# Modulation vectors from transposed weights: row sums on VectorE in place of sums over partitions on TensorE

## The chip, the cores and the metric

The kernel runs on one NeuronCore of a Trainium2 chip (the 1 core that the program uses). The metric is the time of one execution on the device in microseconds. TensorE (PE in the rows) multiplies matrices; its weight loads (PEld) overlap its matmuls. VectorE (DVE) and ScalarE (ACT) work elementwise, GpSimd (POOL) does small work beside them, and SyncE (SP) issues nearly all transfers, in the order of its queue.

## What is computed

A diffusion backbone of two layers over 1024 latent tokens and 256 context tokens of width 1024, all in float32. Each layer has a mixer (attention and spatial gating side by side) and a SwiGLU FFN. What matters here is the modulation: from a condition `c` for the latent tokens and `c_ctx` for the context tokens each layer computes six vectors of 1024, which scale, shift and gate the two sub-layers.

```python
silu_c, silu_cc = silu(c), silu(c_ctx)
for l in range(2):
    m_x = (silu_c  @ w_mod[l] + b_mod[l]).reshape(6, 1024)   # w_mod[l]: 1024 x 6144
    m_c = (silu_cc @ w_mod[l] + b_mod[l]).reshape(6, 1024)
    hx = rms_norm(x, g_pre_mix[l]) * (1 + m_x[1]) + m_x[0]   # scale 1, shift 0
    hc = rms_norm(xc, g_pre_mix[l]) * (1 + m_c[1]) + m_c[0]
    x  = x + m_x[2] * rms_norm(mixer(hx, hc), g_post_mix[l]) # gate 2
    x  = x + m_x[5] * rms_norm(ffn(rms_norm(x, g_pre_ffn[l]) * (1 + m_x[4]) + m_x[3]), g_post_ffn[l])
```

The context stream goes the same way with `m_c`; it is not needed behind the mixer's keys and values in the second layer.

## The kernel before

Activations stand transposed, features on the partitions, as eight blocks (`KT`) of 128x128 for a tile of 128 tokens. Float32 products are made of three matmuls of rounded high and low parts: `rnd` (line 118) rounds a part on ScalarE, `sub_lo` (line 121) and `split_w` (line 377) take the remainder on VectorE. A page (`PG`, 35 of them) is 4 KB of every partition; `BK` are the eight banks of PSUM. A tile's name in the rows ends in `_p` for a page, `_b` for a buffer of four pages and `_k` for a bank.

The vectors for scale and shift must end as columns, in `fm[:, l, v, ...]`: feature on the partition, one column per block, with `v` 0 for latent and 1 for context. The gates must end as rows in device memory, from where they are later spread over all partitions (`load_g`).

The weights `w_mod` lie with the input feature on the partition. `mods_first` (line 169) makes shift and scale of the first layer's mixer before anything else can start: the scale's eight blocks, and one of the shift's, go through TensorE with the two conditions as a two-column stationary operand (two rows in the bank, tile `m_k`); the other seven blocks of the shift are multiplied and added up by VectorE in two accumulators (`macc`, 128 partial sums per feature), and four matmuls with `one_v` sum these over the partitions. Four matmuls of one row put the bias in. The rows are then copied to `mrow`, transposed (`mt_k`) and put into `fm`.

All other vectors are made beside the main work by `mods_steps` (line 224), one job per vector, for one condition or both. A job takes a step when the main loops call `fill`: one weight block of 512 KB is loaded and multiplied by VectorE with a scalar per partition and added to the accumulator (line 235). At the end TensorE sums over the partitions, in tile `mg_k`: for a gate two matmuls of 512 columns with a column of ones as stationary operand, for scale and shift eight matmuls that load the accumulator's 128x128 blocks as weights and multiply them with the column of ones. Float32 matmuls take two passes each. The products' scheduling priority is put back (`late=150`), so that they run where VectorE has room. Jobs of both conditions are the gates and the first mixer vectors of each layer; in the first product of an FFN (`ffn_in`) the jobs have a ring of four pages to themselves (`rings["j"]`, line 1200).

At the start, `norm_early` normalises the two context tiles and transposes them; `norm_late` applies scale and shift (`hte` to `hTc`, high and low). `load_z` brings the first projection's weights (`wraw` to `winh`, `winl`), whose matmuls are `pz_k`. The latent tiles follow in four pairs: `norm_x` (`xs`), eight transposes a tile (`hT_k`), scale and shift (`ht`, line 342), high and low part (`hTl`). In the order of each engine's queue a scheduler decides, by dependencies, priorities and its own costs.

Of the kernel before, what the change touches and what calls it, by code (L numbers as in the profile page):

```python
# [10 lines left out]
F32 = mybir.dt.float32  # L11
F32R = mybir.dt.float32r
I32 = mybir.dt.int32
AF = mybir.ActivationFunctionType
# [18 lines left out]
NDVE = 7  # L33
# [62 lines left out]
def trunk(ctx: ExitStack, tc, x, xctx, w_mod, b_mod, vecs, gqk, gsg, g_post, w_z, w_in, w_sT, w_out,  # L96
# [14 lines left out]
    def mm(o, lhsT, rhs, start, stop):  # L111
        nc.tensor.matmul(o, lhsT, rhs, start=start, stop=stop)  # L112

    def act(o, i, f, **kw):
        A.activation(out=o, in_=i, func=f, **kw)  # L115
# [18 lines left out]
    one_v = cst.tile([P, 2, 2], F32, name="one_v")  # L134
    nc.gpsimd.memset(one_v, 0.0)
    for v in range(2):
        nc.gpsimd.memset(one_v[:, v, v:v + 1], 1.0)
    one2 = cst.tile([1, 2], F32, name="one2")
    nc.gpsimd.memset(one2, 1.0)
# [4 lines left out]
    dma(out=vrow.t[:64, :], in_=vecs)  # L144
    bk = BK.get([512], F32, "vt")
# [4 lines left out]
    act(cT.rearrange("p a b -> p (a b)"), vec[:, 48:64], AF.Silu)  # L150

# [10 lines left out]
    def put_scale(l, v, ffn, src):  # L162
        V.scalar_tensor_tensor(out=fm[:, l, v, 2 * ffn, :], in0=src, scalar=1.0, in1=gpre(l, ffn),
                               op0=ALU.add, op1=ALU.mult)

    def put_shift(l, v, ffn, src):
        V.tensor_copy(out=fm[:, l, v, 2 * ffn + 1, :], in_=src)

    def mods_first():

        parts = (1, 0)
        bks = [[BK.get([512], F32, "m0") for _ in range(2)] for _ in parts]
        row = PG.get([1024], F32, "mrow")
        nc.gpsimd.memset(row.t[:34, :], 0.0)
        for n, p in enumerate(parts):
            b = PG.get([1024], F32, "brow")
            dma(out=b.t[:1, :], in_=b_mod[0, p * D:(p + 1) * D].partition_broadcast(1))
            for h in range(2):
                mm(bks[n][h].t[:2, :], one2, b.t[:1, h * 512:(h + 1) * 512], True, False)
            b.free()  # L180
        accs = [PG.get([1024], F32, "macc") for _ in range(2)]
        for kt in range(KT):
            if kt == NDVE:
                for v in range(2):
                    for h in range(2):
                        mm(bks[1][h].t[:2, :], one_v[:, v, :], accs[v].t[:, h * 512:(h + 1) * 512], False, False)
                    accs[v].free()
            for n, p in enumerate(parts):
                w = PG.get([1024], F32, "wm")
                dma(out=w.t, in_=w_mod[0, kt * P:(kt + 1) * P, p * D:(p + 1) * D])  # L190
                if p == 0 and kt < NDVE:
                    for v in range(2):
                        if kt == 0:
                            V.tensor_scalar(out=accs[v].t, in0=w.t, scalar1=cT[:, v, 0:1], scalar2=None, op0=ALU.mult)
                            continue
                        V.scalar_tensor_tensor(out=accs[v].t, in0=w.t, scalar=cT[:, v, kt:kt + 1], in1=accs[v].t,
                                               op0=ALU.mult, op1=ALU.add)
                else:
                    for h in range(2):
                        mm(bks[n][h].t[:2, :], cT[:, :, kt], w.t[:, h * 512:(h + 1) * 512], False, kt == KT - 1)  # L200
                w.free()
        yield
        with tc.high_priority():
            for n in range(2):
                for h in range(2):
                    o, i = row.t[32 * n:32 * n + 2, h * 512:(h + 1) * 512], bks[n][h].t[:2, :]
                    if h:
                        V.tensor_copy(out=o, in_=i)
                    else:
                        act(o, i, AF.Copy)  # L210
                    bks[n][h].free()
        bt = BK.get([KT, 34], F32, "mt")
        for k in range(KT):
            nc.tensor.transpose(bt.t[:, k, :], row.t[:34, k * P:(k + 1) * P], idn[:34, :34])
        row.free()
        for v in range(2):
            put_scale(0, v, 0, bt.t[:, :, v])
            put_shift(0, v, 0, bt.t[:, :, 32 + v])
        bt.free()
        yield  # L220
# [3 lines left out]
    def mods_steps(l, part, vs, late=150):  # L224
        accs = {}
# [4 lines left out]
        for kt in range(KT):  # L230
            w = jring[0].get([1024], F32, "wm")
            dma(out=w.t, in_=w_mod[l, kt * P:(kt + 1) * P, part * D:(part + 1) * D])
            with tc.high_priority(offset=-late):
                for v in vs:
                    V.scalar_tensor_tensor(out=accs[v].t, in0=w.t, scalar=cT[:, v, kt:kt + 1], in1=accs[v].t,  # L235
                                           op0=ALU.mult, op1=ALU.add)
            w.free()
            yield
        for _ in range(3):
            yield  # L240
        for v in vs:
            if part in (2, 5):
                g = jring[0].get([1024], F32, "gp")
                dma(out=g.t[0:1, :], in_=g_post[l, part // 5, :].partition_broadcast(1))
                for h in range(2):
                    bk = BK.get([512], F32, "mg")
                    mm(bk.t[0:1, :], ones[:, 0:1], accs[v].t[:, h * 512:(h + 1) * 512], True, True)
                    V.scalar_tensor_tensor(out=g.t[0:1, h * 512:(h + 1) * 512], in0=bk.t[0:1, :], scalar=32.0,
                                           in1=g.t[0:1, h * 512:(h + 1) * 512], op0=ALU.mult, op1=ALU.mult)
                    bk.free()  # L250
                d = dr.tile([1, D], F32, name=f"grow{l}{part}{v}")
                dma(out=d, in_=g.t[0:1, :])
                grow[l, part, v] = d
                g.free()
            else:
                bk = BK.get([512], F32, "mg")
# [3 lines left out]
                bk.free()  # L260
            accs[v].free()
        yield
# [39 lines left out]
    def norm_early(xt):  # L302

        xs = norm_x(xt)
# [146 lines left out]
    def gmlp_ln(vp, c0, sgrow, res):  # L451
# [3 lines left out]
        for c in range(2):  # L455
            st = sm.tile([P, 2, 6], F32, name="bnst", tag="bnst")
# [59 lines left out]
    def layer(l):  # L516
# [7 lines left out]
        if not last:  # L524
            hT.make_c()
            early = []
            for i in range(NC):
                xt = load_x(xc_d[i])
                early.append(norm_early(xt.t))
                xt.free()  # L530
            first = mods_first()
            next(first)
            wu += load_z(l, 0, (0, 1))
            next(first)
# [1102 lines left out]
def _layout(inputs):  # L1637
# [12 lines left out]
    w_in = w_in[:, :, 1024:].reshape(DEPTH, KT, P, NPIECE, PC).transpose(0, 3, 2, 1, 4)  # L1650
    w_fi = a["w_ffn_in"].reshape(DEPTH, KT, P, 2, NJ // 2, 2, P).transpose(0, 4, 3, 2, 5, 1, 6)
# [4 lines left out]
        "x": a["x"][0], "xctx": a["ctx"][0], "w_mod": a["w_mod"], "b_mod": a["b_mod"], "vecs": vecs, "gqk": gqk,  # L1656
        "gsg": np.stack([a["g_sg"], a["b_sg"]], 1), "g_post": np.stack([a["g_post_mix"], a["g_post_ffn"]], 1),
# [21 lines left out]
```

## Time and profile before

| what | us |
|---|---|
| median of 3 runs | 2685.35 |
| lowest and highest of them | 2679.77, 2685.67 |
| profiled execution, its own time | 2682.48 |
| its span | 2680.7 |
| TensorE busy (share of the span) | 2631.3 (98%) |
| weight loads of TensorE | 2163.6 (81%) |
| VectorE busy | 2044.2 (76%) |
| ScalarE busy | 1300.0 (48%) |
| GpSimd busy | 642.1 (24%) |

The profile is of one execution. Its span leaves out 1.8 us of its own time. The shares are means over stretches that differ: the start up to about 61 us waits for weights; the mixer, the FFN's first product (from about 680 to 1150 us in the first layer, from 2048 to 2458 in the second) and the FFN's second product follow one another. A matmul's row shows its latency; how many go through is seen from the distance of their starts. Where times are read from a stretch, they are times from the span's start.

### The profile page before, as it was taken

The numbers are of one execution on the slowest core, as the hardware profiler recorded it, in microseconds if no ns is written. First come the engines' busy times: TensorE is split into PE (matmuls) and PEld (weight loads), VectorE is DVE, ScalarE is ACT, GpSimd is POOL, SyncE is SP. The second block draws the span as 40 slices with busy tenths as digits, with TensorE's granted clock in tenths as the row PEclk, the third lists the DMA queues.
The fourth block names the chain that finished last, engine by engine and source line by source line (L and its number), as shares of the span: only waits on it lengthen the run. The fifth ranks groups of instructions, "written<-read, shape, count | busy, mean of one in ns | idle before, by whom it ended". The sixth has DMA issues, their size and how long they took to land. (4 is left out here: it accounts for less than half of the span.)

```text
span 2680.7 us, 35573 instructions
## 1 busy us (share of the span) xinstructions
PE 2631.3 (98%) x13125; PEld 2163.6 (81%) x13125; DVE 2044.2 (76%) x2886; ACT 1300.0 (48%) x2269; POOL 642.1 (24%) x637
## 2 busy tenths in 40 slices
PE   7999999999999999999999999999998999999998
PEld 4789777788888788888899889777787888888886
DVE  7775788857888887677898777888758766667776
ACT  5323788844332323543566323788745333334433
POOL 1112000002233333275010113000014223231746
PEclk9999999999999999999999999999999999999999
DMA  7430001233533333787576631001231422216984
GB/s 291 126 120 33 3 15 28 60 121 115 176 142 141 132 126 134 221 187 201 189 240 210 235 112 64 5 9 48 84 134 79 140 88 95 91 69 207 201 207 173
DMA packets 126458, 338.44 MB, mean 126 GB/s; under 512 B 24302, under 2 KB 25134, under 8 KB 121164
## 3 DMA queue, kind: packets, MB, share of 16 engines
q1 hardware_dynamic: 113612, 313.09, 34.1%
q0 software_dynamic: 12672, 23.07, 5.2%
q8 instruction: 103, 1.69, 0.3%
q14 instruction: 71, 0.58, 0.1%
HBM read 290.32 MB, written 45.71 MB: 125 GB/s over the span
## 5 line engine op out<-in xcount | busy, mean ns | idle before, releaser
L112 PE MATMUL fi_k<-blk_p,fw_p 128*128 128x512 f32 x2640 | 609.3, 390 | 0.7 <-ACT blk_p L118 0.7
L112 PEld LDWEIGHTS fi_k<-blk_p,fw_p 128*128 128x128 f32 x2640 | 496.6, 188 | 106.4 <-issue 1.7
L112 PE MATMUL fo_k<-fs_p,fs_p 128*128 128x512 f32 x1848 | 420.1, 389 | 0.2 <-DVE fs_p L121 0.2
L112 PEld LDWEIGHTS fo_k<-fs_p,fs_p 128*128 128x128 f32 x1848 | 346.6, 188 | 72.5 <-DVE fs_p L121 0.6
L118 ACT ACTIVATE fw_p<-fir_b 128x512 fp32r<-128x512 f32 x200 | 126.0, 631 | 318.4 <-PE fi_k L112 302.3
L112 PE MATMUL pv_k<-sp_b,vt_p 128*128 128x512 f32 (+3 forms) x1008 | 277.4, 392 | 2.8 <-DVE sp_b L121 2.0
L112 PE MATMUL fi_k<-blk_b,fw_p 128*128 128x512 f32 x1056 | 249.1, 392 | 1.1 <-DVE y_p L997 1.1
L121 DVE TENSOR_TENSOR fs_p<-fo_p,fs_p 128x512 fp32r<-128x512 f32 x212 | 191.5, 960 | 60.3 <-ACT fs_p L118 59.6
L112 PEld LDWEIGHTS fi_k<-blk_b,fw_p 128*128 128x128 f32 x1056 | 199.4, 189 | 43.0 <-DVE y_p L997 1.5
L287 POOL TENSOR_SCALAR rs<-ss 128x1 f32<-128x1 f32 x74 | 25.2, 340 | 870.1 <-DVE ss L993 594.4
L121 DVE TENSOR_TENSOR sp_b<-pt_p,sp_b 128x1024 fp32r<-128x1024 f32 (+1 forms) x168 | 200.4, 1196 | 23.1 <-ACT sp_b L118 20.4
L112 PEld LDWEIGHTS pv_k<-sp_b,vt_p 128*128 128x128 f32 (+1 forms) x1008 | 161.7, 170 | 58.2 <-DVE sp_b L121 8.0
L739 DVE TENSOR_REDUCE mx<-ml_k 128x1 f32<-128x512 f32 x256 | 169.1, 685 | 37.3 <-PE ml_k L112 36.6
L118 ACT ACTIVATE fs_p<-fo_p 128x512 fp32r<-128x512 f32 x212 | 119.4, 621 | 144.8 <-POOL fo_p L1273 55.3
L115 ACT ACTIVATE pt_p<-st_k 128x512 f32<-128x512 f32 (+1 forms) x336 | 180.6, 592 | 12.6 <-PE st_k L112 11.4
L121 DVE TENSOR_TENSOR fw_p<-fir_b,fw_p 128x512 fp32r<-128x512 f32 x200 | 178.1, 891 | 10.8 <-ACT fw_p L118 8.6
L235 DVE SCALAR_TENSOR_TENSOR macc_p<-wm_p,cT,macc_p 128x1024 f32<-128x1024 f32 x128 | 171.5, 1358 | 18.5 <-DMA wm_p<-in_w_mod_dram 15.8
L118 ACT ACTIVATE sp_b<-pt_p 128x1024 fp32r<-128x1024 f32 (+1 forms) x168 | 175.9, 1048 | 1.4
L112 PE MATMUL pz_k<-winh_p,hTl_b 128*128 128x512 f32 x512 | 160.7, 391 | 1.8 <-ACT hTl_b L118 1.2
L1110 POOL TENSOR_TENSOR S_p<-fir_b 128x512 f32<-128x512 f32 x40 | 58.1, 1453 | 376.2 <-issue 323.1
L112 PE MATMUL fi_k<-h2c_p,fih_p 128*128 128x256 f32 x704 | 128.0, 284 | 0.0
L112 PEld LDWEIGHTS pz_k<-winh_p,hTl_b 128*128 128x128 f32 x512 | 96.0, 188 | 25.2 <-issue 1.7
(275 smaller groups left out, 5045.8 us busy)
## 6 DMA issues: line engine op xcount, KB each, us to landing
wm_p<-in_w_mod_dram SPq DMA_DIRECT2D x112, 512.0 KB
fir_b<-in_w_fi_dram SPq DMA_DIRECT2D x40, 1024.0 KB
fir_p<-in_w_fi_dram SPq DMA_DIRECT2D x52, 512.0 KB
hid<-hid_p SPq DMA_DIRECT2D x44, 512.0 KB
fo_p<-hid SPq DMA_DIRECT2D x76, 256.0 KB
fo_p<-in_w_fo_dram SPq DMA_DIRECT2D x76, 256.0 KB
fo_p<-in_w_fo_dram POOLq DMA_DIRECT2D x74, 256.0 KB, 6.6
fo_b<-hid SPq DMA_DIRECT2D x56, 256.0 KB
```

The source lines that it names most:

```text
L112: nc.tensor.matmul(o, lhsT, rhs, start=start, stop=stop)
L115: A.activation(out=o, in_=i, func=f, **kw)
L118: A.activation(out=o, in_=i, func=AF.Copy)
L121: V.tensor_tensor(out=o, in0=i, in1=hi.bitcast(F32), op=ALU.subtract)
L235: V.scalar_tensor_tensor(out=accs[v].t, in0=w.t, scalar=cT[:, v, kt:kt + 1], in1=accs[v].t, op0=ALU.mult, op1=ALU.add)
L287: nc.gpsimd.tensor_scalar(out=y, in0=src, scalar1=float(eps), scalar2=1.0, op0=ALU.add, op1=ALU.mult)
L739: V.tensor_reduce(out=mx[:, b, i:i + 1], in_=bk.t, axis=AX.X, op=ALU.max)
L1110: tt_(out=sp.t[:, 0], in0=a21, in1=a22, op=ALU.add)
```

## The change

The weights are laid out transposed by the host: in block `[l, part, k]` the partition is the output feature and the 1024 inputs lie along the row. A condition's silu is spread as a row over all partitions (`crow`). One VectorE operation multiplies a weight block with that row and writes the sum along the row as one column (`accum_out`), straight into `fm` or, for a gate, into the column tile `gcol`. Nothing is left to sum over the partitions.

- `mods_steps`: no accumulator, no memset on GpSimd, no matmuls with ones. The bias, and for a gate also the post-norm's weight, come as columns (`load_cols`, tile `bcol`) and are added by one or two small VectorE operations. A gate's eight columns go through one transpose (128x8 to 8x128, `mg_k`) to become rows for device memory. Each job loads the silu row from device memory to all partitions, 512 KB per condition. With both conditions, the first product of a block goes to a page `prod` of its own and the second overwrites the weight block.
- `mods_first`: the scale's eight blocks stay on TensorE (`w_m1`, laid out as before). Of the shift, six blocks of outputs go to VectorE; two blocks of outputs (`NPE`, 256 columns) go to TensorE in eight matmuls (`w_m0`). The one-row matmuls and those with `one_v` are gone. The silu rows are loaded ahead of all else and passed to device memory for the jobs.
- The transposes of the context tiles, which stood among the two-row matmuls, now come after them (`tc.issue_after`): the first tile's, then those of `mrow`, then the second tile's.
- `bnst` has two buffers in place of four.

```diff
-NDVE = 7
+NPE = 2
@@ trunk
+    crow = [PG.get([1024], F32, "crow") for _ in range(2)]
+    for v in range(2):
+        dma(out=crow[v].t, in_=vecs[48 + 8 * v:56 + 8 * v, :].rearrange("a b -> (a b)").partition_broadcast(P))
...
+    cd = dr.tile([2, D], F32, name="crow")
+    for v in range(2):
+        act(crow[v].t, crow[v].t, AF.Silu)
@@ helpers
+    def load_cols(o, n=1):
+        b = sm.tile([P, 2, KT], F32, name="bcol", tag="bcol", bufs=2)
+        dma(out=b[:, :n], in_=cols[o:o + n].rearrange("n p k -> p n k"))
+        return b
...
+    def mods_block(ring, w, cr, res):
+        for n, c in enumerate(cr):
+            prod = w if n == len(cr) - 1 else ring.get([1024], F32, "prod")
+            V.scalar_tensor_tensor(out=prod.t, in0=w.t, scalar=1.0, in1=c.t, op0=ALU.mult, op1=ALU.mult, accum_out=res[n])
+            if prod is not w:
+                prod.free()
+        w.free()
@@ mods_first
...
+        for kt in range(KT):
+            w = PG.get([1024], F32, "wm")
+            dma(out=w.t, in_=w_m1[kt])
             for h in range(2):
+                mm(bks[h].t[:2, :], cT[:, :, kt], w.t[:, h * 512:(h + 1) * 512], kt == 0, kt == KT - 1)
+            w.free()
+            if kt < KT - NPE:
                 w = PG.get([1024], F32, "wm")
+                dma(out=w.t, in_=w_mod[0, 0, NPE + kt])
+                mods_block(PG, w, crow, [fm[:, 0, v, 1, NPE + kt:NPE + kt + 1] for v in range(2)])
+            elif kt < KT - NPE + 2:
+                o = 4 * (kt - KT + NPE)
+                w = PG.get([4, NPE * P], F32, "wm")
+                dma(out=w.t, in_=w_m0[:, o:o + 4])
+                for k in range(4):
+                    ins = mm(bs_.t[:2, :], cT[:, :, o + k], w.t[:, k], o + k == 0, o + k == KT - 1)
+                w.free()
+        for v in range(2):
+            dma(out=cd[v:v + 1, :], in_=crow[v].t[0:1, :])
+            crow[v].free()
+        yield ins
@@ mods_steps
         for v in vs:
-            accs[v] = jring[0].get([1024], F32, "macc")
-            nc.gpsimd.memset(accs[v].t, 0.0)
-            dma(out=accs[v].t[0:1, :], in_=b_mod[l, part * D:(part + 1) * D].partition_broadcast(1))
-        for kt in range(KT):
+            c = jring[0].get([1024], F32, "crow")
+            dma(out=c.t, in_=cd[v, :].partition_broadcast(P))
+            cr.append(c)
...
             w = jring[0].get([1024], F32, "wm")
-            dma(out=w.t, in_=w_mod[l, kt * P:(kt + 1) * P, part * D:(part + 1) * D])
+            dma(out=w.t, in_=w_mod[l, part, k])
             with tc.high_priority(offset=-late):
-                for v in vs:
-                    V.scalar_tensor_tensor(out=accs[v].t, in0=w.t, scalar=cT[:, v, kt:kt + 1], in1=accs[v].t,
-                                           op0=ALU.mult, op1=ALU.add)
-            w.free()
+                mods_block(jring[0], w, cr, [r[:, k:k + 1] for r in res])
...
             if part in (2, 5):
-                    mm(bk.t[0:1, :], ones[:, 0:1], accs[v].t[:, h * 512:(h + 1) * 512], True, True)
...
+                V.tensor_tensor(out=src, in0=src, in1=b[:, 0], op=ALU.add)
+                V.scalar_tensor_tensor(out=src, in0=src, scalar=32.0, in1=b[:, 1], op0=ALU.mult, op1=ALU.mult)
+                bk = BK.get([P], F32, "mg")
+                nc.tensor.transpose(bk.t[:KT, :], src, idn)
...
             else:
-                for k in range(KT):
-                    mm(bk.t[:, k:k + 1], accs[v].t[:, k * P:(k + 1) * P], ones[:, 0:1], True, True)
-                (put_shift if part in (0, 3) else put_scale)(l, v, part // 3, bk.t[:, :KT])
+                (put_shift if part in (0, 3) else put_scale)(l, v, part // 3, src, b[:, 0])
@@ layer
+            with tc.issue_after(ins.ins):
+                early = [norm_early(xcs[0])]
+                next(first)
+                early.append(norm_early(xcs[1]))
```

On VectorE in the first mixer, before the third pair of latent tiles (`ht_p_622`) gets its scale and shift, this stood before. `macc_p_528` and `macc_p_531` are the accumulators of the first gate; six more products of that gate stand ahead of the first pair.

```order
L235 SCALAR_TENSOR_TENSOR macc_p_528<-wm_p_546,cT,macc_p_528 128x1024
L235 SCALAR_TENSOR_TENSOR macc_p_531<-wm_p_546,cT,macc_p_531 128x1024
L235 SCALAR_TENSOR_TENSOR macc_p_528<-wm_p_664,cT,macc_p_528 128x1024
L235 SCALAR_TENSOR_TENSOR macc_p_531<-wm_p_664,cT,macc_p_531 128x1024
L235 SCALAR_TENSOR_TENSOR macc_p_528<-wm_p_668,cT,macc_p_528 128x1024
L299 TENSOR_SCALAR xs_p_684<-x_p_682,rs 128x1024
L299 TENSOR_SCALAR xs_p_693<-x_p_691,rs 128x1024
L235 SCALAR_TENSOR_TENSOR macc_p_528<-wm_p_672,cT,macc_p_528 128x1024
L235 SCALAR_TENSOR_TENSOR macc_p_531<-wm_p_668,cT,macc_p_531 128x1024
L235 SCALAR_TENSOR_TENSOR macc_p_528<-wm_p_676,cT,macc_p_528 128x1024
L235 SCALAR_TENSOR_TENSOR macc_p_531<-wm_p_672,cT,macc_p_531 128x1024
L235 SCALAR_TENSOR_TENSOR macc_p_531<-wm_p_676,cT,macc_p_531 128x1024
```

At the same place on VectorE stands now this; the third pair's first tile is `ht_p_628`, `crow_p_531` and `crow_p_533` are the silu rows of the two conditions, and two more products stand right ahead of this, two ahead of the first pair.

```order
L180 SCALAR_TENSOR_TENSOR prod_p_548,gcol<-wm_p_546,crow_p_531 128x1024
L180 SCALAR_TENSOR_TENSOR prod_p_553,gcol<-wm_p_551,crow_p_531 128x1024
L180 SCALAR_TENSOR_TENSOR wm_p_546,gcol<-wm_p_546,crow_p_533 128x1024
L180 SCALAR_TENSOR_TENSOR wm_p_551,gcol<-wm_p_551,crow_p_533 128x1024
L180 SCALAR_TENSOR_TENSOR prod_p_672,gcol<-wm_p_670,crow_p_531 128x1024
L180 SCALAR_TENSOR_TENSOR prod_p_677,gcol<-wm_p_675,crow_p_531 128x1024
L180 SCALAR_TENSOR_TENSOR wm_p_670,gcol<-wm_p_670,crow_p_533 128x1024
L180 SCALAR_TENSOR_TENSOR prod_p_682,gcol<-wm_p_680,crow_p_531 128x1024
L180 SCALAR_TENSOR_TENSOR wm_p_675,gcol<-wm_p_675,crow_p_533 128x1024
L312 TENSOR_SCALAR xs_p_694<-x_p_692,rs 128x1024
L180 SCALAR_TENSOR_TENSOR wm_p_680,gcol<-wm_p_680,crow_p_533 128x1024
L180 SCALAR_TENSOR_TENSOR prod_p_687,gcol<-wm_p_685,crow_p_531 128x1024
```

Ten of the sixteen products stood between the second pair and the third before; now it is thirteen, of which these are eleven.

On VectorE again, behind the third pair, before: the last operations of the fourth pair (`ht_p_775`) and the weight splits of the second projection.

```order
L121 TENSOR_TENSOR hTl_b_295<-ht_p_754,hTl_b_295 128x1024
L342 TENSOR_SCALAR ht_p_775<-hT_k_776,fm 128x128
L342 TENSOR_SCALAR ht_p_775<-hT_k_785,fm 128x128 x2
L248 SCALAR_TENSOR_TENSOR gp_p_796<-mg_k_798,gp_p_796 1x512
L377 TENSOR_TENSOR winl_p_888<-wraw_p_885,winh_p_887 128x1024
L121 TENSOR_TENSOR hTl_b_295<-ht_p_775,hTl_b_295 128x1024
L377 TENSOR_TENSOR winl_p_894<-wraw_p_891,winh_p_893 128x1024
L235 SCALAR_TENSOR_TENSOR macc_p_870<-wm_p_873,cT,macc_p_870 128x1024
```

Now, with `ht_p_785` as the fourth pair's last tile and `crow_p_878` as the silu row of the next job:

```order
L262 TENSOR_TENSOR gcol<-gcol,bcol 128x8
L389 TENSOR_TENSOR winl_p_895<-wraw_p_892,winh_p_894 128x1024
L263 SCALAR_TENSOR_TENSOR gcol<-gcol,bcol 128x8
L389 TENSOR_TENSOR winl_p_901<-wraw_p_898,winh_p_900 128x1024
L180 SCALAR_TENSOR_TENSOR wm_p_880,fm<-wm_p_880,crow_p_878 128x1024
L180 SCALAR_TENSOR_TENSOR wm_p_883,fm<-wm_p_883,crow_p_878 128x1024
L180 SCALAR_TENSOR_TENSOR wm_p_886,fm<-wm_p_886,crow_p_878 128x1024
L267 COPY gp_p_812<-mg_k_810 8x128
L354 TENSOR_SCALAR ht_p_785<-hT_k_795,fm 128x128 x2
L267 COPY gp_p_820<-mg_k_818 8x128
L180 SCALAR_TENSOR_TENSOR wm_p_889,fm<-wm_p_889,crow_p_878 128x1024
L121 TENSOR_TENSOR hTl_b_298<-ht_p_785,hTl_b_298 128x1024
```

Where one weight split stood ahead of the last tile's low part, two stand now, and four products of the next job.

## Rows read from the trace of the kernel before

**Rows 1.** The page, busy time of each engine (share of the span), xinstructions.

```profile
PE 2631.3 (98%) x13125; PEld 2163.6 (81%) x13125; DVE 2044.2 (76%) x2886; ACT 1300.0 (48%) x2269; POOL 642.1 (24%) x637
```

**Rows 2.** Busy time by stretch: PE, PEld, DVE, ACT, POOL; clock, DMA share, GB/s.

```profile
61.00:104.00 43.00, 42.42 (x191) 32.08 (x191) 39.84 (x55) 25.05 (x52) 5.81 (x9) 1.00 0.47 150
...
700.00:1060.00 360.00, 360.00 (x1615) 297.19 (x1614) 305.80 (x367) 108.55 (x180) 122.42 (x78) 0.99 0.40 141
1440.00:1700.00 260.00, 259.37 (x1711) 235.01 (x1710) 194.49 (x319) 101.46 (x184) 40.23 (x55) 1.00 0.39 131
2077.00:2141.00 64.00, 64.00 (x283) 52.67 (x283) 50.33 (x64) 21.74 (x37) 18.91 (x13) 1.00 0.38 132
```

**Rows 3.** The tile macc: xcount, duration ns min/median/max, first and last start.

```profile
L112 PEld LDWEIGHTS mg_k<-ones,macc_p x160: 186/192/338, 148.3 to 1642.8; 128*128 128x128 f32 x160
...
L235 DVE SCALAR_TENSOR_TENSOR macc_p<-wm_p,cT,macc_p x128: 1264/1279/2321, 49.3 to 2102.6; 128x1024 f32<-128x1024 f32 x128
...
L112 PE MATMUL mg_k<-macc_p,ones x24: 590/592/593, 87.0 to 2142.1; 128*1 128x512 f32 x24
L228 POOL MEMSET macc_p<- x16: 945/954/961, 32.1 to 2079.9; 128x1024 f32 x16
...
L196 DVE SCALAR_TENSOR_TENSOR macc_p<-wm_p,cT,macc_p x12: 1278/1282/1286, 13.1 to 27.1; 128x1024 f32<-128x1024 f32 x12
```

**Rows 4.** Timeline of PE around one scale group and one gate: start, us, operation.

```profile
147.59 0.62 PE L112 MATMUL pz_k<-winh_p,hTl_b 128*128 128x512 f32 x2
...
148.27 0.39 PE L112 MATMUL pz_k<-winh_p,hTl_b 128*128 128x512 f32 x1
148.50 1.84 PE L112 MATMUL mg_k<-ones,macc_p 128*128 128x1 f32 x16
150.20 0.49 PE L112 MATMUL pz_k<-winh_p,hTl_b 128*128 128x512 f32 x1
...
2140.84 1.88 PE L112 MATMUL mg_k<-macc_p,ones 128*1 128x512 f32 x4
2142.65 2.60 PE L112 MATMUL fi_k<-blk_p,fw_p 128*128 128x512 f32 x10
```

**Rows 5.** Timelines of DVE and PE, the latent tiles of the first mixer.

```profile
51.11 6.06 DVE L235 SCALAR_TENSOR_TENSOR macc_p<-wm_p,cT,macc_p 128x1024 f32<-128x1024 f32 x5
...
60.47 0.50 PE L112 MATMUL pz_k<-winh_p,hTl_b 128*128 128x512 f32 x1 [1.21 <-ACT hTl_b L118]
...
83.20 3.88 PE L335 MATMUL hT_k<-idr,xs_p 128*128 128x128 f32 x32
...
84.94 2.00 DVE L342 TENSOR_SCALAR ht_p<-hT_k,fm 128x128 f32<-128x128 f32 x6
...
95.02 1.20 DVE L377 TENSOR_TENSOR winl_p<-wraw_p,winh_p 128x1024 fp32r<-128x1024 f32 x1
```

**Rows 6.** Timeline of all engines, the start.

```profile
6.55 0.19 ACT L115 ACTIVATION_READ_ACCUMULATOR xs_p<-x_p 128x1 f32 x1
...
10.77 0.60 ACT L115 ACTIVATE hte_p<-hT_k 128x512 f32<-128x512 f32 x1
...
15.87 13.88 PE L112 MATMUL m_k<-wm_p,cT 128*2 128x512 f32 x28
...
29.68 1.06 ACT L118 ACTIVATE winh_p<-wraw_p 128x1024 fp32r<-128x1024 f32 x1 [15.77 <-DMA wraw_p<-in_w_z_dram]
...
33.02 3.60 PE L112 MATMUL m_k<-wm_p,cT 128*2 128x512 f32 x8
...
41.62 0.79 PE L112 MATMUL pz_k<-winh_p,hTc_p 128*128 128x512 f32 x1 [3.48 <-ACT hTc_p L118]
```

**Rows 7.** Busy time by stretch, columns as in rows 2, two pieces of the start.

```profile
16.00:18.00 2.00, 2.00 (x4) 0.34 (x3) 2.00 (x2) 0.00 (x0) 0.00 (x0) 0.64 1.03 418
18.00:20.00 2.00, 2.00 (x3) 0.26 (x2) 1.92 (x3) 0.00 (x0) 0.00 (x0) 0.51 1.02 406
```

**Rows 8.** Waits of the SP queue from 640 to 1150 us: total, times, longest.

```profile
SPq L232 <- DVE macc_p L235: 82.1, 29, 5.8
```

More of the change, by code (lines that the diff above doesn't have):

```diff
@@ L111, in mm @@
     def mm(o, lhsT, rhs, start, stop):
-        nc.tensor.matmul(o, lhsT, rhs, start=start, stop=stop)
+        return nc.tensor.matmul(o, lhsT, rhs, start=start, stop=stop)
     def act(o, i, f, **kw):
@@ L133, in trunk @@
     nc.gpsimd.memset(mhalf, -0.5)
[L134 to L139, printed above, removed]
     vec = cst.tile([P, 64], F32, name="vec")
@@ L169, in mods_first @@
     def mods_first():
-        parts = (1, 0)
-        bks = [[BK.get([512], F32, "m0") for _ in range(2)] for _ in parts]
+        bks = [BK.get([512], F32, "m0") for _ in range(2)]
+        bs_ = BK.get([NPE * P], F32, "m0")
         row = PG.get([1024], F32, "mrow")
         nc.gpsimd.memset(row.t[:34, :], 0.0)
-        for n, p in enumerate(parts):
-            b = PG.get([1024], F32, "brow")
-            dma(out=b.t[:1, :], in_=b_mod[0, p * D:(p + 1) * D].partition_broadcast(1))
+        b0 = load_cols(0, 2)
@@ L202, in mods_first @@
[L202 to L211, printed above, removed]
+                mm(bks[h].t[:2, :], cT[:, :, kt], w.t[:, h * 512:(h + 1) * 512], kt == 0, kt == KT - 1)
@@ new lines, in mods_first @@
+        for v in range(2):
+            dma(out=cd[v:v + 1, :], in_=crow[v].t[0:1, :])
+            crow[v].free()
+        yield ins
+        with tc.high_priority():
+            for h in range(2):
+                o, i = row.t[0:2, h * 512:(h + 1) * 512], bks[h].t[:2, :]
+                if h:
+                    V.tensor_copy(out=o, in_=i)
+                else:
+                    act(o, i, AF.Copy)
+                bks[h].free()
+            act(row.t[32:34, 0:NPE * P], bs_.t[:2, :], AF.Copy)
+            bs_.free()
@@ L216, in mods_first @@
         for v in range(2):
-            put_scale(0, v, 0, bt.t[:, :, v])
-            put_shift(0, v, 0, bt.t[:, :, 32 + v])
+            put_shift(0, v, 0, fm[:, 0, v, 1, NPE:], b0[:, 0], slice(NPE, KT))
+        for v in (1, 0):
+            put_scale(0, v, 0, bt.t[:, :, v], b0[:, 1])
+            put_shift(0, v, 0, bt.t[:, :NPE, 32 + v], b0[:, 0], slice(0, NPE))
         bt.free()
@@ L224, in mods_steps @@
     def mods_steps(l, part, vs, late=150):
-        accs = {}
+        cr = []
         for v in vs:
-            accs[v] = jring[0].get([1024], F32, "macc")
-            nc.gpsimd.memset(accs[v].t, 0.0)
-            dma(out=accs[v].t[0:1, :], in_=b_mod[l, part * D:(part + 1) * D].partition_broadcast(1))
-        for kt in range(KT):
+            c = jring[0].get([1024], F32, "crow")
+            dma(out=c.t, in_=cd[v, :].partition_broadcast(P))
+            cr.append(c)
+        if part in (2, 5):
+            res = sm.tile([P, 2, KT], F32, name="gcol", tag="gcol", bufs=1)
+            res = [res[:, n, :] for n in range(len(vs))]
+        else:
+            res = [fm[:, l, v, 2 * (part // 3) + (part in (0, 3)), :] for v in vs]
@@ L231, in mods_steps @@
+        for k in range(KT):
             w = jring[0].get([1024], F32, "wm")
-            dma(out=w.t, in_=w_mod[l, kt * P:(kt + 1) * P, part * D:(part + 1) * D])
+            dma(out=w.t, in_=w_mod[l, part, k])
             with tc.high_priority(offset=-late):
-                for v in vs:
-                    V.scalar_tensor_tensor(out=accs[v].t, in0=w.t, scalar=cT[:, v, kt:kt + 1], in1=accs[v].t,
-                                           op0=ALU.mult, op1=ALU.add)
-            w.free()
+                mods_block(jring[0], w, cr, [r[:, k:k + 1] for r in res])
@@ L455, in gmlp_ln @@
         for c in range(2):
-            st = sm.tile([P, 2, 6], F32, name="bnst", tag="bnst")
+            st = sm.tile([P, 2, 6], F32, name="bnst", tag="bnst", bufs=2)
             for h in range(2):
@@ L525, in layer @@
             hT.make_c()
-            early = []
+            xcs = []
             for i in range(NC):
                 xt = load_x(xc_d[i])
-                early.append(norm_early(xt.t))
+                xcs.append(norm_x(xt.t))
                 xt.free()
             first = mods_first()
-            next(first)
+            ins = next(first)
             wu += load_z(l, 0, (0, 1))
-            next(first)
+            with tc.issue_after(ins.ins):
+                early = [norm_early(xcs[0])]
+                next(first)
+                early.append(norm_early(xcs[1]))
             for i in range(NC):
```

63 lines of the change are left out of this document (24 added, 39 removed).

## Prediction

> **What bounds the kernel now.** I read the page's busy times first, then the same by stretch, then the rows of the tiles that the change touches, then the timeline around them. TensorE is busy for 98% of the span and VectorE for 76% [rows 1]. By stretch the picture is sharper [rows 2]: from 700 to 1060 us TensorE is busy for 360.00 of 360 us, from 2077 to 2141 for all 64, from 1440 to 1700 for all but 0.6. There, whatever TensorE no longer does is time won, as long as VectorE, with 305.80 of 360 us, does not run full. The exceptions are the start (0 to 61 us: TensorE does two-row matmuls and waits) and 61 to 104 us, where VectorE has 39.84 of 43 us and is nearly as late as TensorE. So three places decide: the start, the stretch to 104 us, and the sums over partitions in the rest.
>
> **TensorE work that goes.** Two kinds of sums [rows 3]. The scale and shift vectors need 160 passes with a full 128x128 weight load each: ten groups of 16. In the timeline of one group [rows 4] matmuls of 512 columns start 0.23 us apart (three in the 0.68 us from 147.59 to 148.27); the next one after the group starts at 150.20 and not at 148.50: 1.70 us lost. The 16 loads of 186 to 192 ns [rows 3] would give 1.9 after the load that each starts behind. I take 1.8: ten groups, **18.0 us**. The gate vectors need 24 passes in 12 matmuls; two of them stand in the timeline from 2140.84 to 2142.65 [rows 4], so 0.905 us each: 12 are **10.9 us**. What comes instead is six transposes of a 128x8 tile. The 32 transposes of 128x128 took 3.88 us [rows 5], 0.12 each: **0.7 us** added; they wait for two short VectorE operations more than the matmuls did. Four of the gate matmuls (3.6 us) lie between 87 and 102 us and are counted with that stretch; outside it the balance is 18.0 + 7.3 - 0.7 = **24.6 us** less, every one of them where TensorE waits for nothing.
>
> **What VectorE gets.** As many products as before in the later jobs (128) and 12 in place of 14 at the start, the same shape with two SBUF inputs: 1.28 us [rows 3]. Each now also writes a sum along its row. No row of before shows a VectorE operation that writes a sum; the nearest is ScalarE's, which shows a separate read of 0.19 us behind the operation [rows 6]. The bounds: nothing extra, and a product that takes twice as long (1.28 us more, as if the sum needed a pass of its own). I take 0.19, the only row with a sum, so 1.47 us for each. For 64 products between 700 and 1060 us that is 12.2 us on 305.80: 318 of 360, still 42 us free, so I cost it at nothing; without that cover it is 12.2 us. Between 1440 and 1700 and at 2077 VectorE has more room [rows 2].
>
> [...]
>
> **What else moves.** GpSimd loses 16 memsets of 0.95 us [rows 3], off the path. SP loses 16 loads of 4 KB and gets 16 broadcast loads of 512 KB (the silu rows) and small columns, and two broadcasts more at the start: 9.4 MB in all. Eight of them fall in 700 to 1060 us at a DMA share of 0.40 [rows 2]: covered. In jobs with two vectors the ring of four pages now holds two rows, one product and one weight block, so a block's load waits until the step before has used its page. SP already waits there for VectorE (82.1 us in 29 waits [rows 8]); behind it stand weight loads of the next pair, issued a pair (14 products) ahead. Nothing, by that lead; if it failed, TensorE would wait in the middle of its fullest stretch.
>
> **The start.** Before: the two-row matmuls begin at 15.87 us, the last of them end at 36.6 (33.02 + 3.60), and the first z matmul starts at 41.62 us [rows 6]. The granted clock fell to 0.64 and 0.51 between 16 and 20 us, and the DMA queues were full, at 406 to 418 GB/s [rows 7]. 52 passes go down to 32 of 512 columns and 16 of 256; by the 0.43 us of a pass, from eight in 3.60 us with the tail of the last left off, that is about 17 us for 22, so TensorE now waits for the weights. These come later by the two broadcasts: 1.05 MB at some 410 GB/s is 2.6 us. The first z block ends its load in 29.68 us before [rows 6], behind the last weight block; I put the last weight block now at about 31 us, the two-row matmuls' end at 33. But ScalarE has the hte copies, which stood at 10.77 before, and two weight roundings in front of the first hTc: some 5 us of work after fm is there at about 35.5. First z matmul at about 40.5: 1 us won. Then 48 z matmuls, the transposes, first latent z matmul 1 to 2 us before 60.47 [rows 5].
>
> **61 to 104 us.** Before, 16 products stand in front of the ht operations of the third pair of latent tiles (84.94 us [rows 5]); now 15 of the 16, with only two of them ahead of the first pair. At 1.47 us they are 22.1 us against 19.4 us at 1.21 (6.06 us for five [rows 5]), 2.7 us more than before. The last operation of the fourth pair now stands behind four products of the next job and two weight splits, 4 x 1.47 + 2 x 1.20 = 8.3 us, where one split of 1.20 stood [rows 5]: 7.1 us more. So the 3.6 us of gate matmuls and the 1 to 2 us of the start are spent waiting for VectorE here. I count **nothing** won or lost by 104 us. The ends: 6 us won, if a sum costs nothing and 4 us of the waits go; 8 us lost, if those products also wait for their blocks.
>
> **Sum.** The profiled run took 2682.48 us; less 24.6 is 2657.9. The median of the three runs is 2.9 us above the profiled one: **2661 us**, a gain of 0.9%. A difference under 0.3% (8 us) can't be told from no change.
>
> **Rivals.** [...]
> (b) The sums go, but VectorE passes its own lateness on: 12.2 us in the full stretch and 7.1 us at the fourth pair: 2661 + 19 = 2680, no change that can be told. For it: 39.84 of 43 us between 61 and 104 [rows 2]; against: 42 us free in the long stretch. That TensorE's passes were hidden anyway would end here too, but the matmuls behind them are pushed back [rows 4].
> (c) Slower: the product with a sum takes 2.56 us. Between 700 and 1060 us 64 x 1.28 = 82 us meet 54 free: 28 us over. At the start 12 x 2.56 = 31 us from about 11 us on, so fm waits for VectorE at 42 and not for TensorE at 34, 8 us; 15 products before the third pair cost 19 more, less what the sum above already has for them (2.7). 2661 + 28 + 8 + 16 = 2713, less what the later starts hide of each other, some 8 us: 2705. It decides as soon as a product costs about 0.9 us more. For it: no row has such a product; against: the read on ScalarE is 0.19 us.
>
> **How the numbers follow.** Forecast 0.64 (2654 to 2670 by the ends of the stretch to 104 us and of the 1.7 to 1.9 us); (a) 0.10, around 2673; (b) 0.12, 2677 to 2693; (c) 0.11, 2694 to 2712; a better start than I see, 0.03, 2645 to 2654. Faster by over 0.3%: 0.64 + 0.10 + 0.03 = 0.77; within it 0.12; slower 0.11. The range goes from 2647 to 2684: the forecast, (a), half of (b) and most of the better start.
>
> **What would show it.** Products of 1.28 us with a read of 0.1 to 0.2 us behind each; no rows on mg but six transposes; TensorE busy for all of 700 to 1060 us shifted left; a first z matmul near 40.5 us; DVE busy for about 318 us in the long stretch. [...]

## Result and profile after

The changed kernel takes 2652.9 us (median) against 2683.0: a ratio of 0.989, interval 0.9877 to 0.9903, so 30 us or 1.1% less. The profiled run took 2652.54 us with a span of 2650.8; before it was 2682.48 with 2680.7.

The page's busy row, to read beside [rows 1], then the stretches of [rows 2] in the same columns:

```profile
PE 2594.6 (98%) x12943; PEld 2141.2 (81%) x12943; DVE 2040.1 (77%) x3038; ACT 1299.7 (49%) x2270; POOL 620.4 (23%) x617
```

```profile
61.00:104.00 43.00, 39.89 (x188) 33.11 (x187) 40.48 (x76) 23.26 (x49) 4.76 (x8) 0.96 0.65 215
...
700.00:1060.00 360.00, 358.08 (x1573) 293.98 (x1572) 310.27 (x443) 110.78 (x188) 115.15 (x73) 1.00 0.43 152
1440.00:1700.00 260.00, 257.74 (x1629) 229.38 (x1628) 192.85 (x344) 111.87 (x198) 35.36 (x52) 1.00 0.34 118
2077.00:2141.00 64.00, 64.00 (x284) 52.88 (x283) 46.75 (x64) 20.51 (x34) 23.00 (x16) 1.00 0.28 107
```

TensorE is busy for 36.7 us less and still fills the long stretch, where VectorE grew by 4.5 us only, but for waits that it did not have before; the row gives their total in us, their number and the longest:

```profile
PE fi_k L112 <- DVE fw_p L121: 1.8, 5, 0.5
```

The tile of the silu rows, to be read against the products in [rows 3]; the columns are count, duration in ns (min/median/max), first and last start. Below them stand three rows of VectorE's timeline:

```profile
L180 DVE SCALAR_TENSOR_TENSOR wm_p<-wm_p,crow_p x102: 1171/1221/2321, 14.1 to 2076.8; 128x1024 f32<-128x1024 f32 x102
L180 DVE DVE_READ_ACCUMULATOR wm_p<-wm_p,crow_p x102: 70/81/88, 15.3 to 2077.9; 128x1 f32 x102
```

```profile
71.58 1.22 DVE L180 SCALAR_TENSOR_TENSOR prod_p<-wm_p,crow_p 128x1024 f32<-128x1024 f32 x1
72.72 0.08 DVE L180 DVE_READ_ACCUMULATOR prod_p<-wm_p,crow_p 128x1 f32 x1
72.72 1.22 DVE L180 SCALAR_TENSOR_TENSOR prod_p<-wm_p,crow_p 128x1024 f32<-128x1024 f32 x1
```

A product takes 1.22 us and a read 0.08 us, and the next product starts together with the read, 1.14 us behind the one before: no more than the 1.28 us of a product without a row sum before, of which five in a row started 1.20 us apart (6.06 us less the last 1.28, by four [rows 3, 5]). Now the places where the 30 us went. The times are first starts from the tile view of TensorE; the last column is the prediction's sum, split by place.

| stretch | before, us | after, us | won | predicted |
|---|---|---|---|---|
| start to the first latent z matmul | 60.5 | 59.3 | 1.2 | 1 to 2 |
| to the first key/value matmul | 114.5 | 113.1 | 1.4 | 1.8 less 0.2, and 0 by 104 us |
| key/value stage | 42.7 | 33.0 | 9.7 | 1.8 |
| queries, attention, output projection, to the first fi matmul | 445.6 | 447.6 | -2.0 | 0 |
| fi of the first layer | 436.8 | 423.2 | 13.6 | 14.4 less 0.2 |
| to the second layer's z | 405.3 | 406.9 | -1.6 | 0 |
| z, key/value, queries of the second layer | 187.0 | 181.6 | 5.4 | 5.4 less 0.1 |
| attention and output projection | 335.4 | 337.5 | -2.1 | 0 |
| fi of the second layer | 430.5 | 427.4 | 3.1 | 1.8 less 0.1 |
| to the end | 222.4 | 221.2 | 1.2 | 0 |

By these starts fi of the first layer ran from 663 to 1100 us before, not from about 680 to 1150 as said ahead of the prediction. Where the sum has a term, the stretch came out within 1.5 us of it, but for one, the key/value stage, which gave 9.7 us and not 1.8. (Stretches without an edit differ by 1 to 2 us either way, and each column is one execution.) The stage's end is the last latent pkv matmul, of before and then of after:

```profile
L112 PE MATMUL pkv_k<-winh_p,hTl_b x128: 280/283/437, 180.8 to 217.7; 128*128 128x256 f32 x128
```

```profile
L112 PE MATMUL pkv_k<-winh_p,hTl_b x128: 281/283/352, 178.2 to 205.4; 128*128 128x256 f32 x128
```

The timeline of before shows a wait there that none of the rows ahead of the prediction holds. SP issues the last 512 KB block of the key/value weights at 191.03 us, ScalarE rounds it when it has landed, VectorE splits it, and behind the split in VectorE's queue stands the operation on `vt_p` for which TensorE waits 4.72 us. Of after, the same load goes out at 184.38 us, and no such wait follows:

```profile
191.03 0.33 SPq L385 DMA_DIRECT2D wraw_p<-in_w_in_dram  x1
...
195.69 1.06 ACT L118 ACTIVATE winh_p<-wraw_p 128x1024 fp32r<-128x1024 f32 x1 [6.98 <-DMA wraw_p<-in_w_in_dram]
...
196.78 1.23 DVE L377 TENSOR_TENSOR winl_p<-wraw_p,winh_p 128x1024 fp32r<-128x1024 f32 x1 [3.13 <-ACT winh_p L118]
...
200.17 0.42 DVE L121 TENSOR_TENSOR vt_p<-pkv_k,vt_p 128x256 fp32r<-128x256 f32 x1
...
200.74 0.44 PE L112 MATMUL pkv_k<-winh_p,hTl_b 128*128 128x256 f32 x1 [4.72 <-DVE vt_p L121]
```

```profile
184.38 0.33 SPq L397 DMA_DIRECT2D wraw_p<-in_w_in_dram  x1
...
188.11 1.06 ACT L118 ACTIVATE winh_p<-wraw_p 128x1024 fp32r<-128x1024 f32 x1 [1.47 <-DMA wraw_p<-in_w_in_dram]
```

The load waits for a page that one of the job's products holds, by the waits of SP before (total, times, longest):

```profile
SPq L385 <- DVE macc_p L235: 9.0, 1, 9.0
```

The products' scheduling priority is put back by 150, and a job has fewer instructions now; that this moved them ahead is the likely reading. The second experiment shows that the place matters. That the number of instructions moved it is not shown by itself: groups_back, below, has the load late again, but groups_spread, which puts back as many matmuls, has it 11.7 us behind the stage's first matmul, as after (12.0; before 16.0).

Second, the clock. TensorE by stretch before (busy of 2 us, instructions, granted clock, DMA share, GB/s):

```profile
209.00:211.00 2.00, 2.00 (x19) 1.00 0.00 0
211.00:213.00 2.00, 2.00 (x12) 0.53 0.00 0
213.00:215.00 2.00, 2.00 (x13) 0.62 0.54 158
...
970.00:972.00 2.00, 2.00 (x21) 1.00 1.00 422
972.00:974.00 2.00, 2.00 (x13) 0.57 0.98 387
974.00:976.00 2.00, 2.00 (x7) 0.50 0.48 172
976.00:978.00 2.00, 2.00 (x6) 0.50 0.64 229
978.00:980.00 2.00, 2.00 (x8) 0.72 0.01 2
```

TensorE is busy throughout, and yet the granted clock falls to 0.50, within or right behind the groups of single-column matmuls at 208.68 and 969.94 us. By busy time times the clock that is missing, this costs 1.7 and 3.4 us. In the profiled run after the change every fall of the clock has a wait ahead of it (at 40, 87, 278, 1999 and 2016 us; waits of 4.16, 3.11, 0.91, 3.59 and 3.05 us). So the 13.6 us of fi in the first layer agree with the forecast's 14.2 partly by luck: 3.4 of them are the clock.

### The profile page after: what moved, and what is told of

The parts are those of the page before. It is cut to its first block, busy times and chain, and to the rows that moved or that the text cites. A ratio compares the mean times of both kernels' runs of the same rounds, so it can differ in the third digit from the quotient of the medians.

```text
span 2650.8 us, 35272 instructions
## 1 busy us (share of the span) xinstructions
PE 2594.6 (98%) x12943; PEld 2141.2 (81%) x12943; DVE 2040.1 (77%) x3038; ACT 1299.7 (49%) x2270; POOL 620.4 (23%) x617
## 5 line engine op out<-in xcount | busy, mean ns | idle before, releaser
L180 DVE SCALAR_TENSOR_TENSOR wm_p<-wm_p,crow_p 128x1024 f32<-128x1024 f32 x102 | 130.6, 1292 | 24.4 <-DMA crow_p<-crow 12.8
```

The source lines that it names most:

```text
L180: V.scalar_tensor_tensor(out=prod.t, in0=w.t, scalar=1.0, in1=c.t, op0=ALU.mult, op1=ALU.mult, accum_out=res[n])
```

## Experiments

**The sums of scale and shift, put back.** The identity stands for the accumulator, and the column of sums for the ones:

```diff
@@ mods_steps, for scale and shift, ahead of put_shift/put_scale
+                bk = BK.get([512], F32, "mg")
+                for k in range(KT):
+                    mm(bk.t[:, k:k + 1], idn, src[:, k:k + 1], True, True)
+                bk.free()
```

> The changed kernel with the ten groups of single-column matmuls put back on TensorE at the places where they stood (eight matmuls, 16 passes with a full 128x128 weight load each, against the identity; their result is used by nothing). Theory (a group costs the 1.8 us that its loads take, nothing hides it): 10 x 1.8 = 18 us more than the 2653 us of the changed kernel, so 2671 us, and VectorE's rows stay as they are. Rival (TensorE's time was not the main thing; the gain came from a different order on VectorE and from waits): less than 8 us more, 2653 to 2661 us.

Measured: 2680.6 us, ratio 0.9983 (0.9973 to 0.9992). Against the changed kernel (0.9891 in its later series) that is 25 us, more than the 18 expected and far from the rival's 8. The load of the last block is back at 189.90 us, with a wait of 3.1 us at pkv, and the clock falls without a wait in three places (to 0.50, at 208, 973 and 1041 us). One of them, TensorE by stretch:

```profile
1038.00:1040.00 2.00, 2.00 (x16) 1.00 0.00 0
1040.00:1042.00 2.00, 2.00 (x17) 0.84 0.00 0
1042.00:1044.00 2.00, 2.00 (x10) 0.50 0.00 0
1044.00:1046.00 2.00, 2.00 (x6) 0.50 0.04 2
1046.00:1048.00 2.00, 2.00 (x7) 0.50 0.00 0
```

So the passes matter, and something beside their time.

**The kernel before, with products ahead in one place.**

```diff
-        jobs.append(mods_steps(0, part, vs_))
+        jobs.append(mods_steps(0, part, vs_, 30 if part == 4 else 150))
```

> The kernel before with one number changed: the five last products of the job for the scale of the second sublayer stand up to five rows further ahead on VectorE, so that the page of one of them comes free earlier for the last 512 KB block of the key and value weights, which SP issued at 191.03 us. No TensorE work is taken away. Theory (the 4.7 us that TensorE waits at 195.8 us, and the low clock twice until 215 us, came from that place in VectorE's order, and the change moved it by the way): the wait goes and with it most of the 8 us in that stretch, so 2675 to 2679 us against 2683. Rival (the wait comes from something else, as the sums themselves): 2683 us and the wait stays.

Measured: 0.9981 (0.9973 to 0.999), 5 us less than before without a single matmul taken away. The load goes out 13.6 us behind the stage's first matmul (16.0 before), the wait shrinks to 1.1 us, the granted clock is 1.00 from 195 to 220 us, and the stage takes 36.6 us and not 42.7. So some 6 us of the gain come from VectorE's order and not from the sums. They hold the fall of the clock at 211 us too: the group is still whole here, and TensorE by stretch (12 us) shows no fall behind it:

```profile
206.45 1.91 PE L112 MATMUL mg_k<-ones,macc_p 128*128 128x1 f32 x16
```

```profile
205.00:217.00 12.00, 12.00 (x108) 1.00 0.33 123
```

**Both together.** The two edits above, on the changed kernel.

> The changed kernel with the ten groups of single-column matmuls put back, as in groups_back, and in addition the products of the job for the scale of the second sublayer placed ahead on VectorE, as in before_piece_early. groups_back lost 25 us where ten groups of 1.8 us are 18; there SP issued the last block of the key and value weights at 189.90 us (184.38 in the changed kernel) and TensorE waited 3.1 us at pkv again, with the low clock behind it. Theory (the 7 us beyond the groups are that wait, brought back because the added instructions shifted VectorE's order): wait and low clock go, 18 us over the changed kernel remain, 2671 to 2674 us. Rival (a group costs 2.5 us by itself): no more than 2 us better than groups_back, 2678 us or more.

Measured: 0.9978 (0.9968 to 0.9988), 1 us better than groups_back: by total time the rival's outcome. The wait at pkv is gone, but the products now stand ahead of the keys' split, and TensorE waits 2.2 us for `kst` instead, with the clock at 0.89 from 195 to 220 us. The edit moved the wait; it could not tell a group's own price. The group of this stage, at 206.92 us, is again without a fall of the clock behind it.

**The same passes in pairs.** `back` (its lines are left out here) holds the matmuls of groups_back, two of the eight for each vector of the job.

```diff
@@ mods_steps
...
-        for _ in range(3):
-            yield
+        for i in range(3):
+            back((2 * i, 2 * i + 1))
+            yield
+        back((6, 7))
```

> The changed kernel with the same 160 single-column passes back on TensorE as in groups_back, but two matmuls (four passes) at a time with other matmuls between, and with VectorE's products around the key and value stage in the order of the changed kernel. In groups_back the clock fell to 0.5 at 208 to 212, 973 to 977 and 1041 to 1049 us although TensorE had not waited: 6.8 us, each time within or right behind a run of 16 or 32 single-column passes, as in the kernel before at 211 to 215 and 972 to 980 us (5.1 us). Theory (18 us are the passes themselves, the rest is the clock that falls behind a whole group, and the wait at pkv): without whole groups no such fall and no wait, 18 us over the changed kernel, 2671 to 2674 us. Rival (a pass costs more than its load, whatever its neighbours): 25 us over it as in groups_back, 2678 us or more.

Measured: 2669.5 us, 0.9946 (0.9931 to 0.996): 15 us above the changed kernel, 10 below groups_back with the same 160 passes. Two stretches of TensorE, of groups_back and then of groups_spread:

```profile
900.00:1060.00 160.00, 160.00 (x720) 0.97 0.40 142
195.00:215.00 20.00, 16.88 (x121) 0.83 0.22 80
```

```profile
900.00:1060.00 160.00, 160.00 (x739) 1.00 0.42 148
195.00:215.00 20.00, 20.00 (x173) 1.00 0.30 106
```

No wait at pkv, and no fall of the clock but behind waits. Ten groups cost 15 us as passes; the other 10 came with the whole groups, as the clock that falls behind some of them, and as the wait. How much of the 10 is which, the totals don't tell; by the trace of groups_back the three falls are 6.8 us, and the wait with the fall behind it 4.6.

**The gates' matmuls, put back.**

```diff
@@ mods_steps, for a gate
+                for h in range(2):
+                    bk = BK.get([512], F32, "mg")
+                    mm(bk.t[0:1, :].rearrange("o (r c) -> o r c", r=4), src[:, h:h + 1],
+                       idn.unsqueeze(1).broadcast_to([P, 4, P]), True, True)
+                    bk.free()
```

> The changed kernel with the 12 one-row matmuls of the gate vectors put back on TensorE (512 columns each, two passes, against the identity; result used by nothing). Theory: 12 x 0.905 = 10.9 us, of which the four between 87 and 102 us (3.6 us) stand beside waits for VectorE and cost little: 7 to 11 us more than 2653, so 2660 to 2664 us. Rival (they ran in time that TensorE had free): under 3 us more, 2653 to 2656 us.

Measured: 2663.2 us, 0.9921 (0.9907 to 0.9935): 8 us above the changed kernel, within the 7 to 11 of the theory. By the trace the four in the stretch to the first key/value matmul are not cheap, though: that stretch takes 3.6 us more than in the changed kernel (116.7 against 113.1).

**Each product twice.**

```diff
@@ mods_block, in the later jobs
+            V.scalar_tensor_tensor(out=prod.t, in0=prod.t, scalar=0.0, in1=c.t, op0=ALU.mult, op1=ALU.mult,
+                                   accum_out=spare[:, n:n + 1])
```

> The changed kernel with every product of the later jobs done a second time on VectorE (same shape, with a sum; its result is used by nothing): 128 x 1.27 = 163 us more work on VectorE, 64 x 1.27 = 81 us of them between 700 and 1060 us, where 48 are free (310 of 358 busy). Theory of the third rival (above the free time it comes through): about 81 - 48 = 33 us there and 15 x 1.27 less 2.7 = 16 us before the third pair at 61 to 104 us, 40 to 50 us more than 2653, so 2693 to 2703 us. Other theory (the products yield to everything else and move on to the stretch behind, where VectorE has time): under 20 us more, 2653 to 2673 us.

Measured: 2721.4 us, 1.0138 (1.0122 to 1.0155): 67 us above the changed kernel, more than either theory had. The z tiles lose 12 us, the key/value stage 12, and fi of the first layer 42. From 700 to 1060 us, and TensorE's waits there:

```profile
700.00:1060.00 360.00, 338.73 (x1457) 274.51 (x1456) 340.84 (x506) 99.74 (x171) 121.12 (x68) 0.99 0.40 143
```

```profile
PE fi_k L112 <- DVE fw_p L121: 21.3, 15, 3.5
```

VectorE is busy for 341 of 360 us there and TensorE has lost 21, all of it in waits for weight splits on VectorE. So the free time isn't free to the last microsecond.

**Products without a sum.** `accum_out` is left out in the later jobs, and a constant stands in place of the sums.

> The changed kernel with the products of the later jobs writing no sum along the row (the sums are left out of the computation and replaced by a constant). Theory (the sum costs a short read of 0.08 us behind each product and nothing inside it): the product stays at 1.22 us, VectorE is 128 x 0.05 to 0.08 = 6 to 10 us less busy in all, the total stays within 2 us of 2653. [...]

Measured: 0.9882 (0.9868 to 0.9896), the same as the changed kernel. The product takes 1.22 us without the sum too, and VectorE is busy for 309.05 us in the long stretch against 310.27: 0.02 us for each of 64. The 6 to 10 us less in all that the theory had did not show: 2033.4 us against 2040.1 in the changed kernel's first trace and 2033.7 in its second.

**Context transposes early.** `issue_after` is taken out, and both `norm_early` calls go ahead of `mods_first`.

> The changed kernel with the transposes of the context rows not held behind the last two-row matmul: they run at the start, as in the kernel before. Theory (from 33.7 to 40.5 us TensorE waits for ScalarE, which copies the transposed rows there; copied earlier, the first z matmul comes 1 to 2 us sooner, but by 104 us VectorE sets the pace): first z matmul at 38.5 to 39.5 us, total within 2 us of 2653. Rival (the transposes and their copies stand in the way of the two-row matmuls at the start, which is why they were moved): first z matmul at 41 us or later, total 1 to 3 us more.

Measured: first z matmul at 38.3 us (40.5 in the changed kernel), and total 0.9892 (0.9879 to 0.9906), the same. The 2.2 us are lost by the first key/value matmul, which starts at 173.1 against 172.4 us.

**The start of before with the later jobs of the change.**

> The start of the kernel before (52 two-row passes more or less as they were, the first job's sums on TensorE, context transposes early, the two silu rows loaded behind the weights) with the later jobs of the changed kernel. Theory (the start gave 1.2 us at the first latent z matmul and VectorE takes that back by 104 us): within 2 us of the changed kernel, 2652 to 2656 us. Rival (the start is where the unexpected gain lies): 5 us or more above it, 2658 us or more.

Measured: 2656.8 us, 0.9894 (0.9878 to 0.9911). The median is 0.8 us above the range that the theory gave, the ratio that of the changed kernel: the start is not where the gain lies.

**Fewer products ahead of the third pair.** On top of context_turn_early:

```diff
-                    fill(4)
+                    fill(3)
```

> The changed kernel with the context transposes early (as in context_turn_early, which won 2 us at the first z matmul and lost them again by 104 us) and three in place of four product steps after each pair of z tiles, so that fewer products stand ahead of the third pair on VectorE. Theory (VectorE sets the pace from 61 to 104 us): TensorE's wait of 3.1 us at 84.8 us goes, and the 2 us of the start are kept: 2647 to 2650 us. Rival (the products collide with the key and value stage from 175 us on, where VectorE is late too): no gain there or 2 to 6 us more, 2653 to 2660 us.

Measured: 2648.0 us, 0.9862 (0.9848 to 0.9875): the best of all, 7 us below the changed kernel's 2654.5 in the series after it. TensorE from 61 to 104 us:

```profile
61.00:104.00 43.00, 41.63 (x198) 34.17 (x197) 38.88 (x69) 24.46 (x49) 5.24 (x8) 1.00 0.47 147
```

It is busy for 41.6 us and not 39.9, at the full clock and not 0.96, and the first key/value matmul starts at 167.1 and not 172.4 us. Two steps in place of three, and the changed kernel once more:

> As fewer_products_early (2648 us), with two in place of three product steps after each pair of z tiles: TensorE's waits in 61 to 104 us are already nearly gone there, so theory: no more than 1 us better at 104 us, and the products that go to the key and value stage bring a wait there, 2648 to 2653 us. Rival (VectorE has time in the later stages): 2645 to 2647 us.

> The changed kernel once more, as it is, to stand beside the others of this series: 2653 us, ratio to the kernel before 0.989.

Measured: 2652.9 us, 0.9883 (0.9868 to 0.9898), and 2654.5 us, 0.9891 (0.9874 to 0.9908). With two steps the wait comes back from 84 us on, in other places: TensorE waits for `ht` and for ScalarE's `u` in the z stage, and the first key/value matmul is at 174.1 us. The rival falls, and the theory too in where it put the loss.

## Why the prediction was right, and where it was off

**The sign and the cause held.** The sums over partitions were on TensorE's path: put back, they cost 15 us as passes and 8 us for the gates, 23 of the 30. The sum had 18.0 and, beyond the first stretch, 7.3. The 1.8 us of a group was taken between one gap of 1.70 [rows 4] and 1.9 from the loads. The second bound does not follow from its row: 16 loads of 0.19 us [rows 3] are 3.0 us end to end, and it is because they overlap that the 16 of one group take 1.98 us together:

```profile
148.27 1.98 PEld L112 LDWEIGHTS mg_k<-ones,macc_p 128*128 128x128 f32 x16
```

In pairs a group costs 1.5. Part of the difference is that TensorE has waits of its own now, which passes that are put back can fill: fi waits 1.8 us for weight splits on VectorE in the changed kernel and 0.4 us in groups_spread. The prediction had put VectorE's cost there at nothing; such waits came, and they are small: 1.9 us of the 14.4.

**Two terms were missing, both gains.** First, the stretches that were read left out the one from 104 to 215 us; there TensorE was busy for 106.3 of 111 us, and the 4.7 us of waiting hung on a page held by a product. The change moved that product. Before_piece_early shows that the 6 us were to be had without the change. Second, the clock behind a group: the granted clock at 211 and 972 us before (0.50) shows 5.1 us more to win, of which the 1.7 at 211 us are among those 6. Groups_spread shows none of these falls with the passes kept and the groups split; why some whole groups have one and others don't stays open. Against these stand some 6 us lost in three stretches without an edit, where the prediction had 0. In the first of them the clock falls to 0.50 at 278 to 286 us, 3.3 us by itself, behind two short waits at the start of attention. Before has the same two waits, of 0.91 and 0.76 us at 289.59 and 292.26 us, at the full clock; before_piece_early and the second trace of the changed kernel have them with the fall, gates_back and half_products_early without. So neither the waits nor the change decide it; what does was not tested. That gains and losses which the sum did not have left 5 us between them is luck: the mechanism was right, and the total is nearer than the terms.

**The product.** 1.47 us was assumed, with the read of ScalarE as nearest row [rows 6]; it is 1.22 and 0.08, from start to start 1.15 us over three in a row (71.58 to 75.02 us), a little less than before. VectorE stands at 310 us in the long stretch and not at 318. Rival (c), the doubled product, is out. Its 2.56 us was the author's upper bound, twice the product of before, and no run shows it: with two float32 sources the median product takes 1.22 us with the sum (after) and 1.22 us without it (products_no_sum). Had the rival come true, the price of 2705 was too low: products_twice lost 42 us in fi where the rival had 28, and 12 more in the key/value stage, which it had at nothing.

**The start.** The first z matmul was put at 40.5 us and came at 40.52; the two-row matmuls ended at 33.7 (33 predicted), and the clock did not fall between 16 and 20 us, as it had to 0.64 and 0.51 in [rows 7]. The chances have 2673 for (a), a start at the lower clock; no run shows it: from 14 to 34 us the granted clock was 1.00 after the change and in every experiment. From 33.7 us on, the path is ScalarE's, as predicted: early transposes made it 2 us shorter.

**61 to 104 us.** "Nothing won or lost" held: 1.2 us were won by 60 us, and the context's last z matmuls start 0.8 us earlier than before at 123 us. The 3.6 us of gate matmuls became a wait of 3.11 us and a fall of the clock (0.50 at 88 to 90 us): VectorE, behind 15 products, comes to `ht` of the third pair at 85.36 us, ScalarE rounds it at 86.82, and TensorE waits for that. The timeline of after:

```profile
85.36 2.64 DVE L354 TENSOR_SCALAR ht_p<-hT_k,fm 128x128 f32<-128x128 f32 x8
...
86.82 1.06 ACT L118 ACTIVATE hTl_b<-ht_p 128x1024 fp32r<-128x1024 f32 x1
...
87.93 0.80 PE L112 MATMUL pz_k<-winh_p,hTl_b 128*128 128x512 f32 x1 [3.11 <-ACT hTl_b L118]
```

Rival (b), lateness passed on by VectorE, is true for this place and, with 1.8 us, for fi. Fewer_products_early shows that it was worth 6 us by the first key/value matmul (167.1 us against 173.1 in context_turn_early, from which it differs in one number).

## What to carry over

Read every stretch in which the bounding engine waits, not only those that the edit touches: an edit on one engine can move work of another engine that a scheduler places by priority. On TensorE, price a run of tiny matmuls by its loads and by the granted clock behind it: here the 16 loads of one group took 1.98 us, and behind some groups a clock of 0.50 cost 1.7 or 3.4 us more. Products that can wait should not stand ahead of the tiles that TensorE needs next; here one number, with the context transposes early, was worth 7 us on top of the change.

## What the runs showed of the hardware

- TensorE's granted clock fell to 0.50 while it was busy without a gap: within or behind 16 or 32 passes of one column with a full weight load each, at 211 and 972 us before, at 208, 973 and 1041 in groups_back, at 1040 and 1637 in groups_back_ahead, at 971 in before_piece_early; 1.7 or 3.4 us were lost each time. Not behind every group (at 766, 833 and 1042 us before there was none, nor at 206 in before_piece_early), and in the trace of groups_spread, with four to eight passes at a time, never.
- A row sum on VectorE cost next to nothing on 128x1024 float32: a read of 0.08 us is shown, but the next operation starts with it (both at 72.72 us after), and in busy time it is 0.02 us (309.05 us in products_no_sum against 310.27 after, over 64 products).
- With VectorE busy for 341 of 360 us, TensorE lost 21 of 360 us to it (products_twice).
